# p loaded whole on two queues, zeros multiplied until it is there, the first product in passes, x scaled ahead of the evictions: the start and the end of a decoder block

## The chip, the cores and the metric

The kernel runs on one core of a Trainium2 chip. The core has a matrix engine (TensorE: PE for its products, PEld for its weight loads), a vector engine (DVE), a scalar engine (ACT), a general engine (POOL) and an engine that only issues transfers (SP). Transfers are issued from the queues of SP, ACT and POOL and share 16 DMA engines. The metric is the time of one execution on the device in microseconds (us): the median of several runs, lower is better.

## The reference

One layer of a hybrid decoder block on 512 rows (tokens) of 1024 numbers, in 32-bit floats. In short:

```python
hn = rmsnorm(x, g_mix)                                  # x: (512, 1024)
proj = hn @ w_in                                        # w_in: (1024, 14344), split into 13 parts
(xa, ba, ca, za, q, k, v, o, zb, ig, fg, ga, gb) = split(proj)
ya = ba * causal_short_conv(ca * xa, conv_w, conv_b)    # branch a
ya = (ya * silu(za)) @ w_a_out
hb = mlstm_chunkwise(q, k, v, ig + b_i, fg + b_f)       # branch b, 4 heads
yb = (sigmoid(o) * rmsnorm(hb, g_head) * silu(zb)) @ w_b_out
x = x + (sigmoid(ga) * ya + sigmoid(gb) * yb) @ w_o
gate = sigmoid(rmsnorm(x, g_ple) @ w_ple_gate)
x = x + gate * (p @ w_ple)                              # p: (512, 256), w_ple: (256, 1024)
return rmsnorm(x, g_final)
```

The change touches three pieces of it: the product `p @ w_ple`, which needs nothing but inputs and is computed first; the first rmsnorm of x; and the last rmsnorm with the stores of the result.

## The kernel before, in words

Every product is done in split precision: an operand becomes a high part (ACT copies it into a rounded type) and a low part (DVE or POOL subtracts the high part from the original), and each product is three matmuls, high by high, high by low and low by high (`mm3`, L205 to L207). Weights come in pieces of 128 x 4 x 512 numbers, 1 MB, in four buffers `wraw`, and are split into `whi` and `wlo` on the way (`split_half`, L152 and L153). The order of work on PE, ACT, DVE and POOL is written out by hand: each engine executes its instructions in the order of the program, and waits are put in where data or buffers ask for them. SP's queue holds the loads, each waiting for its buffer. SP and ACT share eight completion semaphores for their transfers, so the ninth transfer is issued only when the first has landed.

The start goes like this. `p` (tile `pin`, four row blocks t of 128 rows, 256 columns) is transposed on PE, in two halves k of 128 columns (`turn_p`, L485), split into `pT`, and multiplied with w_ple. w_ple is piece 0 of the weights; it comes in four quarters q = 2n + k, where n is the half of the 1024 output columns and k the half of the 256 rows. Each quarter is split on its own (`split_quarter`, L522 and L523): before the change the first two low parts are made on DVE and the other two on POOL. The product makes four banks of results for n = 0 (one per row block t), each of six matmuls, three per k. They are copied out to `ple` by `keep_ple` (L511 on DVE, L513 on ACT), and then the four banks are used again for n = 1; the first matmul into a bank waits for the copy out of it. Meanwhile x comes in four row blocks: ACT squares and sums each (`square_x`, L489), DVE and POOL form the reciprocal root (`power_x`, L492 and L493), and DVE scales the block in place (`scale_x`, L497 to L499). After the product with w_ple the scaled x is transposed (`turn_x`, L504) and split into `hn_hi` and `hn_lo`, the left operand of everything that follows. One matmul group of w_ple, (k = 1, t = 3) of n = 1, is kept for later and fills a wait between the transposes of x.

In the end, the last product gives the gate in column halves, the last row block (t = 3) in two quarter pieces. For each row block the gate is applied (`gated`, L1133 to L1135), the squares are summed (`squares`, L1138), the root is formed (`power` on DVE and POOL, L1164 and L1165; `final_scale`, L1169 to L1171), and both halves are scaled and stored (`final`, L1178 to L1183). All eight stores are issued on SP's queue.

Of the kernel before, what the change touches and what calls it, by code (L numbers as in the profile page):

```python
# [14 lines left out]
P = 128  # L15
S = 512
# [20 lines left out]
def hybrid_block(ctx, tc, x, p, g_mix, w_in, conv_w, conv_b, w_a_out, b_gates, g_head,  # L37
# [92 lines left out]
    def load_raw(between=None):  # L130
        i = state["raw"]
        state["raw"] += 1
        raws[i] = wraw.tile([P, HC, CW], F32, name=f"wraw{i}", tag="wraw")
        for src, ks, cs in chunks[i]:
            nc.sync.dma_start(raws[i][:, ks, cs], src)
            if between:
                between = between()
# [71 lines left out]
    def cut(hi, lo, src, scale=None):  # L209

        if scale is None:
            act.activation(hi, src, AF.Copy)
            dve.tensor_tensor(lo, src, hi.bitcast(F32), ALU.subtract)
        else:
            act.activation(hi, src, AF.Copy, scale=scale)
            dve.scalar_tensor_tensor(lo, src, scale, hi.bitcast(F32), ALU.mult, ALU.subtract)
# [226 lines left out]
    start_ctx, sp = open_pool("start")  # L443
    pin = sp.tile([P, NT, PLE], F32, name="pin", tag="hsf0", align_bytes=256)

    def load_p(k):
        nc.sync.dma_start(pin[:, :, k * P:(k + 1) * P],
                          p[0, 0, :, k * P:(k + 1) * P].rearrange("(t p) c -> p t c", p=P))

    load_p(0)  # L450
    load_raw(lambda: load_p(1))
# [8 lines left out]
    xin = sp.tile([P, NT, D], F32, name="xin", tag="xin")  # L460
    hnf = sp.tile([P, KT, S], F32, name="hnf")
    sq = hnf[:, 0:2, :].rearrange("p k s -> p (k s)")
    for t in range(NT):
        nc.sync.dma_start(xin[:, t, :], x[0, t * P:(t + 1) * P, :])
    nc.sync.dma_start(prow[0:8, :], g_mix[0].rearrange("(c p) -> c p", p=P))
    nc.sync.dma_start(prow[8:32, :], conv_w[0].rearrange("j (c p) -> (j c) p", p=P))
    nc.sync.dma_start(prow[32:40, :], conv_b[0].rearrange("(c p) -> c p", p=P))
    nc.sync.dma_start(prow[40:56, :], g_head[0].rearrange("(c p) -> c p", p=P))
    nc.sync.dma_start(prow[56:64, :], g_ple[0].rearrange("(c p) -> c p", p=P))
    load_raw()  # L470
    nc.sync.dma_start(wg_raw, w_in_v[:, :, IG:IG + 2 * NH])
    nc.sync.dma_start(bg, b_gates[0].rearrange("(g h) -> h g", g=2))

    prm = const.tile([P, 64], F32, name="prm")
    gm = prm[:, 0:8]
# [6 lines left out]
    def turn_p(k):  # L482
        pt = ps_x.tile([P, S], F32, name="ptp", tag="x")
        for t in range(NT):
            pe.transpose(pt[:, t * P:(t + 1) * P], pin[:, t, k * P:(k + 1) * P], ident)  # L485
        return pt

    def square_x(t):
        act.activation(sq, xin[:, t, :], AF.Square, accum_out=ss[:, t:t + 1])  # L489

    def power_x(t):
        dve.tensor_scalar(tmp[0][:, t:t + 1], ss[:, t:t + 1], 1.0 / D, EPS, ALU.mult, ALU.add)  # L492
        pool.tensor_tensor(tmp[1][:, t:t + 1], tmp[0][:, t:t + 1], mhalf[:, :1], ALU.pow)  # L493
# [25 lines left out]
    def split_quarter(q, e_lo):  # L519
        hi, lo = (u[:, q % HH, :] for u in splits[0][q // HH])  # L520
        raw = raws[0][:, q, :]
        act.activation(hi, raw, AF.Copy)  # L522
        e_lo.tensor_tensor(lo, raw, hi.bitcast(F32), ALU.subtract)  # L523

    for k in range(2):
        ptp = turn_p(k)
        split_quarter(k, dve)
        cut(pT[0][:, k, :], pT[1][:, k, :], ptp)
    split_quarter(2, pool)
    split_quarter(3, pool)  # L530
    state["split"] = 2
    del raws[0]
    for t in range(3):
        square_x(t)
    whi, wlo = ([splits[0][q // HH][u][:, q % HH, :] for q in range(4)] for u in range(2))
    state["use"] = 1
    splits.pop(0)
# [1 line left out]
    def ple_part(ps, n, k, t):  # L539
        mm3(ps, [u[:, k, t * P:(t + 1) * P] for u in pT], [whi[2 * n + k], wlo[2 * n + k]], k == 0, k == 1)  # L540

    pss = [bank(t) for t in range(NT)]
    for k in range(2):
        for t in range(NT):
            ple_part(pss[t], 0, k, t)
    for t in range(3):
        keep_ple(t, 0, pss[t], True)
        if t < 2:
            power_x(t)
    keep_ple(3, 0, pss[3])  # L550
    square_x(3)
    scale_x(0)
    power_x(2)
    scale_x(1)
    power_x(3)
    scale_x(2)
    scale_x(3)
    pss = [bank(t) for t in range(NT)]
    for k, t in [(0, 0), (0, 1), (0, 2), (0, 3), (1, 0), (1, 1), (1, 2)]:
# [613 lines left out]
    def final(t, n, on_act=False):  # L1173

        y = temp("sv"[n], "y")
        f = fs[:, t:t + 1]
        if n:
            dve.scalar_tensor_tensor(y, xr[:, t, half[1]], f, gfin[:, half[1]], ALU.mult, ALU.mult)  # L1178
# [4 lines left out]
        nc.sync.dma_start(out[0, t * P:(t + 1) * P, half[n]], y)  # L1183
# [27 lines left out]
    gated(pss[3][:, :CW // 2], 3, q[0])  # L1211
    squares(3, q[0], 1)
    final_scale(2)
    gated(psl[:, :CW // 2], 3, q[1])
    squares(3, q[1], 2)
    dve.tensor_scalar(base[:, 3:4], fss[:, 3, 1:2], 1.0 / D, base[:, 3:4], ALU.mult, ALU.add)
    final(2, 0)
    power(3, 2)
    final(2, 1)
    final_scale(3)  # L1220
    final(3, 0, True)
    final(3, 1)
# [23 lines left out]
```

## Time and profile before

| | |
|---|---|
| median of three runs | 870.08 us (869.50 to 870.92) |
| profiled execution, its own time | 871.68 us |
| its span | 869.7 us |
| PE busy | 852.3 us, 98% of the span |
| DVE, ACT, POOL busy | 599.8, 468.4, 255.8 us |
| bytes moved | 169.65 MB, mean 195 GB/s |
| PE's first product with w_ple | at 6.93 us |
| PE's last product | starts at 860.56 us |

The times in the rows that follow are microseconds from the start of the span. A row gives the start, the length, the engine, the line of the kernel, the operation, what it writes and reads, and, in brackets, how long the engine stood before it and what ended that. A matmul's length is its latency; what it costs in a row of matmuls is the distance to the next start. In the list of waits a row gives who waited for whom: the total, the number of waits and the longest. In the tables by stretch, each engine has its busy time and the number of instructions, then come the clock that TensorE was granted, the share of the DMA engines' time and GB/s.

### The profile page before, as it was taken

What the parts mean: (1) busy time and instruction counts of PE and PEld (TensorE: products, weight loads), DVE (VectorE), ACT (ScalarE), POOL (GpSimd) and SP (SyncE); (2) the same over time, 40 slices, a digit from 0 to 9 for tenths busy, and PEclk for the clock granted to TensorE, in tenths of its full rate; (3) what the DMA queues carried; (4) which work ended last, traced back from release to release, by engine and by line L of the source; (5) the groups of instructions that cost most, each with busy time, mean ns of one, the idle gap of its engine ahead of it and who ended that gap; (6) DMA issues with size and microseconds to landing.
All of it is one profiled execution on the core that took longest, in us unless ns stands there. A gap on an engine that the chain in (4) does not pass through costs nothing.

```text
span 869.7 us, 11799 instructions
## 1 busy us (share of the span) xinstructions
PE 852.3 (98%) x4507; PEld 732.3 (84%) x4507; DVE 599.8 (69%) x774; ACT 468.4 (54%) x674; POOL 255.8 (29%) x246
## 2 busy tenths in 40 slices
PE   7999999999999999999999999999999999999995
PEld 6877888888888888888888999999998888788885
DVE  4769676774674666755785588898986777864465
ACT  5575676555563755547656555545453256534342
POOL 3742422322333132331331424333410224030031
PEclk9999999999999999999999999999999999999999
DMA  8799996968855887867869989899898588994002
GB/s 289 262 210 220 275 221 127 223 233 193 177 163 145 191 176 158 238 193 158 236 122 269 230 192 163 202 181 181 181 326 309 97 194 211 272 329 157 1 1 97
DMA packets 100728, 169.65 MB, mean 195 GB/s; under 512 B 6272, under 2 KB 44224, under 8 KB 99392
## 3 DMA queue, kind: packets, MB, share of 16 engines
q0 software_dynamic: 39312, 76.03, 45.1%
q1 hardware_dynamic: 60208, 90.78, 31.5%
q10 hardware_dynamic: 1152, 2.10, 0.7%
q8 instruction: 35, 0.57, 0.3%
q14 instruction: 21, 0.17, 0.1%
HBM read 153.16 MB, written 15.73 MB: 194 GB/s over the span
## 4 chain that ended last, share of the span: by engine, by line
PE 80%; DMA 6%; issue 4%; DVE 4%; ACT 2%; POOL 2%; POOLq 0%; SPq 0%; DVEq 0%; ACTq 0%
PE mm L206 24%; PE mm L207 24%; PE mm L205 24%; DMA wraw<-in_w_in 3%; DMA wraw<-in_w_b_out 2%; DVE wlo L153 2%; PE pv L205 1%; ACT whi L152 1%; PE pv L206 1%; PE pv L207 1%; POOL wraw L159 1%; PE pty L744 1%; DMA sg_d<-c 1%; DMA pin<-in_p 0%; PE sc L207 0%
## 5 line engine op out<-in xcount | busy, mean ns | idle before, releaser
L153 DVE TENSOR_TENSOR wlo<-wraw,whi 128x1024 fp32r<-128x1024 f32 x234 | 299.1, 1281 | 127.3 <-ACT whi L152 127.0
L152 ACT ACTIVATE whi<-wraw 128x1024 fp32r<-128x1024 f32 x236 | 247.0, 1054 | 105.2 <-PE mm L207 44.7
L159 POOL DMA_DIRECT2D wraw<-in_w_in x110 | 136.0, 1402 | 289.1 <-DVE wlo L153 218.5
L205 PE MATMUL mm<-hn_hi,whi 128*128 128x256 f32 (+1 forms) x320 | 105.1, 328 | 0.0
L207 PE MATMUL mm<-hn_hi,wlo 128*128 128x256 f32 (+1 forms) x320 | 104.4, 326 | 0.2 <-POOL wlo L153 0.2
L206 PE MATMUL mm<-hn_lo,whi 128*128 128x256 f32 (+1 forms) x320 | 104.2, 326 | 0.0
L206 PE MATMUL mm<-wlo,hs 128*128 128x512 f32 x256 | 100.7, 393 | 1.1 <-DVE wlo L153 1.0
L205 PE MATMUL mm<-whi,hs 128*128 128x512 f32 x256 | 101.0, 394 | 0.3 <-DVE c L325 0.3
L207 PE MATMUL mm<-whi,hs 128*128 128x512 f32 x256 | 100.2, 391 | 0.0
L321 ACT ACTIVATE s<-mm 128x512 f32<-128x512 f32 x78 | 46.4, 595 | 94.6 <-PE mm L207 94.5
L206 PE MATMUL mm<-wlo,hn_hi 128*128 128x512 f32 x192 | 74.9, 390 | 0.2 <-DVE wlo L153 0.2
L205 PE MATMUL mm<-whi,hn_hi 128*128 128x512 f32 x192 | 75.0, 391 | 0.0
L207 PE MATMUL mm<-whi,hn_lo 128*128 128x512 f32 x192 | 74.8, 389 | 0.0
L207 PE MATMUL mm<-hs,wlo 128*128 128x256 f32 x256 | 72.5, 283 | 0.8 <-DVE wlo L153 0.8
L205 PE MATMUL mm<-hs,whi 128*128 128x256 f32 x256 | 72.5, 283 | 0.0
L206 PE MATMUL mm<-hs,whi 128*128 128x256 f32 x256 | 72.4, 283 | 0.0
L207 PEld LDWEIGHTS mm<-hn_hi,wlo 128*128 128x128 f32 x320 | 60.9, 190 | 5.7 <-POOL wlo L153 0.8
L206 PEld LDWEIGHTS mm<-hn_lo,whi 128*128 128x128 f32 x320 | 60.9, 190 | 4.7
L205 PEld LDWEIGHTS mm<-hn_hi,whi 128*128 128x128 f32 x320 | 60.9, 190 | 4.6
L206 PEld LDWEIGHTS mm<-wlo,hs 128*128 128x128 f32 x256 | 48.5, 190 | 11.9 <-DVE wlo L153 2.4
L205 PEld LDWEIGHTS mm<-whi,hs 128*128 128x128 f32 x256 | 48.5, 189 | 10.8 <-DVE c L325 0.7
L207 PEld LDWEIGHTS mm<-whi,hs 128*128 128x128 f32 x256 | 48.5, 189 | 10.1
(276 smaller groups left out, 1680.0 us busy)
## 6 DMA issues: line engine op xcount, KB each, us to landing
wraw<-in_w_in SPq DMA_DIRECT2D x32, 1024.0 KB, 6.1
wraw<-in_w_in POOLq DMA_DIRECT2D x62, 512.0 KB, 6.8
wraw<-in_w_in SPq DMA_DIRECT2D x48, 512.0 KB, 4.5
wraw<-in_w_in POOLq DMA_DIRECT2D x48, 256.0 KB, 5.8
wraw<-in_w_b_out SPq DMA_DIRECT2D x8, 1024.0 KB, 6.4
wraw<-in_w_b_out POOLq DMA_DIRECT2D x16, 512.0 KB, 7.4
yt_d<-yc POOLq DMA_DIRECT2D x4, 1024.0 KB, 7.6
wraw<-in_w_a_out SPq DMA_DIRECT2D x4, 1024.0 KB, 8.9
```

Of the source, the lines that this page charges most:

```text
L152: act.activation(hi, t, AF.Copy)
L153: (e_lo or dve).tensor_tensor(lo, t, hi.bitcast(F32), ALU.subtract)
L159: nc.gpsimd.dma_start(raws[to][:, ks, cs], src[:, ks, :], accum_op=ALU.add)
L205: pe.matmul(ps, lhsT=a[0], rhs=b[0], start=first, stop=False, **kw)
L206: pe.matmul(ps, lhsT=a[0], rhs=b[1], start=False, stop=False, **kw)
L207: pe.matmul(ps, lhsT=a[1], rhs=b[0], start=False, stop=last, **kw)
L321: act.activation(to[i], src, AF.Copy, scale=scale)
L744: pe.transpose(pts[v][:, t * P:(t + 1) * P], y[:, t, v * P:(v + 1) * P], ident)
```

## The change

At the start, p is loaded whole as two transfers of two row blocks each, one on SP's queue and one on ACT's, ahead of everything else. The first transposed half of `hn_lo`, not used yet, is filled with zeros by DVE, and PE multiplies these zeros six times into a spare bank ahead of the transposes of p, and once more after them. w_ple's quarters 0 and 1 are loaded next, then x's blocks 0 and 1, w_ple's quarters 2 and 3, and x's blocks 2 and 3. The seven small loads (five parameter vectors, the gate columns of w_in, the gate biases) move from SP's queue to POOL's. For k = 0 of n = 0 the product is done pass by pass: four matmuls of high by high, four with the low part of p, four with the low part of w_ple. The high part of p's first half is made on DVE instead of ACT, and all four low parts of w_ple on DVE. x's blocks 0 and 1 are squared by ACT before w_ple's quarters 2 and 3 are split, and scaled by DVE before the banks of n = 0 are copied out. At the end, outputs that ACT makes are stored from ACT's queue; the right half of row block 2 is finished before the last quarter of the gate, and its left half moves to ACT.

```diff
+    p_v = p[0, 0].rearrange("(t p) c -> p t c", p=P)
+    for i, queue in enumerate((nc.sync, nc.scalar)):
+        queue.dma_start(pin[:, 2 * i:2 * i + 2, :], p_v[:, 2 * i:2 * i + 2, :])
...
+    def load_ple(n):
+        for src, ks, cs in chunks[0][2 * n:2 * n + 2]:
+            nc.sync.dma_start(raws[0][:, ks, cs], src)
+
+    load_ple(0)
+
+    dve.memset(hn_lo[:, 0, :].bitcast(F32), 0.0)
+    warm = ps_x.tile([P, S], F32, name="warm", tag="x")
+
+    def keep_warm(n):
+        for _ in range(n):
+            pe.matmul(warm, lhsT=hn_lo[:, 0, :P], rhs=hn_lo[:, 0, :], start=True, stop=True)
+
+    keep_warm(6)
...
-    for t in range(NT):
-        nc.sync.dma_start(xin[:, t, :], x[0, t * P:(t + 1) * P, :])
-    nc.sync.dma_start(prow[0:8, :], g_mix[0].rearrange("(c p) -> c p", p=P))
...
+    for i in range(2):
+        for t in range(2 * i, 2 * i + 2):
+            nc.sync.dma_start(xin[:, t, :], x_v[:, t, :])
+        if i == 0:
+            load_ple(1)
     load_raw()
...
+    nc.gpsimd.dma_start(prow[0:8, :], g_mix[0].rearrange("(c p) -> c p", p=P))
...
+    nc.gpsimd.dma_start(wg_raw, w_in_v[:, :, IG:IG + 2 * NH])
+    nc.gpsimd.dma_start(bg, b_gates[0].rearrange("(g h) -> h g", g=2))
...
-    for k in range(2):
-        ptp = turn_p(k)
-        split_quarter(k, dve)
-        cut(pT[0][:, k, :], pT[1][:, k, :], ptp)
-    split_quarter(2, pool)
-    split_quarter(3, pool)
...
+    ptp = turn_p(0)
+    dve.tensor_copy(pT[0][:, 0, :], ptp)
+    hi, lo, raw = quarter(0)
+    act.activation(hi, raw, AF.Copy)
+    low(pT[0][:, 0, :], pT[1][:, 0, :], ptp)
+    low(hi, lo, raw)
+    ptp = turn_p(1)
+    keep_warm(1)
+    split_quarter(1, dve)
+    cut(pT[0][:, 1, :], pT[1][:, 1, :], ptp)
+    for t in range(2):
+        square_x(t)
+        power_x(t)
+    for q in (2, 3):
+        split_quarter(q, dve)
+    for t in range(2):
+        scale_x(t)
...
-    for k in range(2):
+    for i, (a, b) in enumerate(((pT[0], whi), (pT[1], whi), (pT[0], wlo))):
         for t in range(NT):
-            ple_part(pss[t], 0, k, t)
+            pe.matmul(pss[t], lhsT=a[:, 0, t * P:(t + 1) * P], rhs=b[0], start=i == 0, stop=False)
+    for t in range(NT):
+        ple_part(pss[t], 0, 1, t)
+    square_x(2)
     for t in range(3):
         keep_ple(t, 0, pss[t], True)
-        if t < 2:
-            power_x(t)
+        if t == 0:
+            power_x(2)
...
-        nc.sync.dma_start(out[0, t * P:(t + 1) * P, half[n]], y)
+        (nc.scalar if on_act else nc.sync).dma_start(out[0, t * P:(t + 1) * P, half[n]], y)
...
     final_scale(2)
+    final(2, 1)
     gated(psl[:, :CW // 2], 3, q[1])
+    final(2, 0, True)
     squares(3, q[1], 2)
     dve.tensor_scalar(base[:, 3:4], fss[:, 3, 1:2], 1.0 / D, base[:, 3:4], ALU.mult, ALU.add)
-    final(2, 0)
     power(3, 2)
-    final(2, 1)
```

Two places show how this moves instructions. The first is DVE in the start, from its second low part of p on (`pT`, the second one) to its second copy out of a bank (`COPY ple`); `wlo` is a low part of w_ple, `rtmp` are the small columns of the reciprocal root, `xin` is x. Before:

```order
L213 TENSOR_TENSOR pT_135<-ptp,pT_134 128x512
L511 COPY ple_144<-mm 128x512
L492 TENSOR_SCALAR rtmp_141<-ss 128x1
L511 COPY ple_145<-mm 128x512
L492 TENSOR_SCALAR rtmp_141<-ss 128x1
L511 COPY ple_146<-mm 128x512
L497 SCALAR_TENSOR_TENSOR rtmp_143<-rtmp_142,rtmp_141 128x1
L498 TENSOR_SCALAR rtmp_143<-rtmp_143 128x1
L499 TENSOR_SCALAR xin<-xin,rtmp_142,rtmp_143 128x1024
```

And now:

```order
L213 TENSOR_TENSOR pT_141<-ptp,pT_140 128x512
L510 TENSOR_SCALAR rtmp_147<-ss 128x1 x2
L541 TENSOR_TENSOR wlo_181<-wraw_129,whi_180 128x512 x2
L515 SCALAR_TENSOR_TENSOR rtmp_149<-rtmp_148,rtmp_147 128x1
L516 TENSOR_SCALAR rtmp_149<-rtmp_149 128x1
L517 TENSOR_SCALAR xin<-xin,rtmp_148,rtmp_149 128x1024
L515 SCALAR_TENSOR_TENSOR rtmp_149<-rtmp_148,rtmp_147 128x1
L516 TENSOR_SCALAR rtmp_149<-rtmp_149 128x1
L517 TENSOR_SCALAR xin<-xin,rtmp_148,rtmp_149 128x1024
L529 COPY ple_150<-mm 128x512
L510 TENSOR_SCALAR rtmp_147<-ss 128x1
L529 COPY ple_151<-mm 128x512
```

Between the last low part of p and the first copy out of a bank DVE now has two small steps, two low parts of w_ple and two scalings of x, where before it had nothing. On ACT the squares of x's first two blocks (`hnf,ss<-xin`) have moved ahead of the last two splits of w_ple (`whi`), which those low parts need. ACT in the start before, and after it now:

```order
L522 ACTIVATE whi_170<-wraw_128 128x512
L212 ACTIVATE pT_134<-ptp 128x512
L522 ACTIVATE whi_170<-wraw_128 128x512
L212 ACTIVATE pT_134<-ptp 128x512
L522 ACTIVATE whi_172<-wraw_128 128x512 x2
L489 ACTIVATE hnf,ss<-xin 128x1024 x3
L513 ACTIVATE ple_147<-mm 128x512
```

```order
L448 DMA pin<-in_p 128x2x256
L553 ACT_TABLE_LOAD
L553 ACTIVATE whi_178<-wraw_129 128x512
L540 ACTIVATE whi_178<-wraw_129 128x512
L212 ACTIVATE pT_140<-ptp 128x512
L507 ACTIVATE hnf,ss<-xin 128x1024 x2
L540 ACTIVATE whi_180<-wraw_129 128x512 x2
L507 ACTIVATE hnf,ss<-xin 128x1024 x2
L531 ACTIVATE ple_153<-mm 128x512
```

The second place is ACT in the end, from the sigmoid of the last quarter (`e<-mml`) on; `c,fss<-xr` are the squares, `y<-xg` is an output. Before:

```order
L1133 ACTIVATE e<-mm,er 128x256
L1138 ACTIVATE c,fss<-xr 128x256
L1133 ACTIVATE e<-mml,er 128x256
L1138 ACTIVATE c,fss<-xr 128x256
L1180 ACTIVATE y<-xg,fs 128x512
```

And now:

```order
L1167 ACTIVATE e<-mm,er 128x256
L1172 ACTIVATE c,fss<-xr 128x256
L1167 ACTIVATE e<-mml,er 128x256
L1214 ACTIVATE y<-xg,fs 128x512
L1217 DMA out<-y 128x512
L1172 ACTIVATE c,fss<-xr 128x256
L1214 ACTIVATE y<-xg,fs 128x512
L1217 DMA out<-y 128x512
```

An output and its store now stand ahead of the last squares, and the last store of ACT's output follows on ACT's own queue.

More of the change, by code (lines that the diff above doesn't have):

```diff
@@ L444, in hybrid_block @@
     pin = sp.tile([P, NT, PLE], F32, name="pin", tag="hsf0", align_bytes=256)
[L446 to L451, printed above, removed]
+    p_v = p[0, 0].rearrange("(t p) c -> p t c", p=P)
+    for i, queue in enumerate((nc.sync, nc.scalar)):
+        queue.dma_start(pin[:, 2 * i:2 * i + 2, :], p_v[:, 2 * i:2 * i + 2, :])
+    state["raw"] = 1
+    raws[0] = wraw.tile([P, HC, CW], F32, name="wraw0", tag="wraw")
+    def load_ple(n):
[8 more added lines that the diff above has]
+    keep_warm(6)
     pT = [sp.tile([P, 2, S], F32R, name=f"pT{i}", tag="pT" if i else "hsf1", align_bytes=256) for i in range(2)]
@@ L462, in hybrid_block @@
     sq = hnf[:, 0:2, :].rearrange("p k s -> p (k s)")
-    for t in range(NT):
-        nc.sync.dma_start(xin[:, t, :], x[0, t * P:(t + 1) * P, :])
-    nc.sync.dma_start(prow[0:8, :], g_mix[0].rearrange("(c p) -> c p", p=P))
[L466 to L469, printed above, removed]
-    load_raw()
-    nc.sync.dma_start(wg_raw, w_in_v[:, :, IG:IG + 2 * NH])
-    nc.sync.dma_start(bg, b_gates[0].rearrange("(g h) -> h g", g=2))
+    x_v = x[0].rearrange("(t p) d -> p t d", p=P)
+    for i in range(2):
[3 more added lines that the diff above has]
+            load_ple(1)
+    load_raw()
+    nc.gpsimd.dma_start(prow[0:8, :], g_mix[0].rearrange("(c p) -> c p", p=P))
+    nc.gpsimd.dma_start(prow[8:32, :], conv_w[0].rearrange("j (c p) -> (j c) p", p=P))
+    nc.gpsimd.dma_start(prow[32:40, :], conv_b[0].rearrange("(c p) -> c p", p=P))
+    nc.gpsimd.dma_start(prow[40:56, :], g_head[0].rearrange("(c p) -> c p", p=P))
+    nc.gpsimd.dma_start(prow[56:64, :], g_ple[0].rearrange("(c p) -> c p", p=P))
+    nc.gpsimd.dma_start(wg_raw, w_in_v[:, :, IG:IG + 2 * NH])
+    nc.gpsimd.dma_start(bg, b_gates[0].rearrange("(g h) -> h g", g=2))
     prm = const.tile([P, 64], F32, name="prm")
@@ L523, in split_quarter, with quarter, low @@
         e_lo.tensor_tensor(lo, raw, hi.bitcast(F32), ALU.subtract)
-    for k in range(2):
-        ptp = turn_p(k)
-        split_quarter(k, dve)
-        cut(pT[0][:, k, :], pT[1][:, k, :], ptp)
-    split_quarter(2, pool)
-    split_quarter(3, pool)
+    def quarter(q):
+        hi, lo = (u[:, q % HH, :] for u in splits[0][q // HH])
+        return hi, lo, raws[0][:, q, :]
+    def low(hi, lo, src):
+        dve.tensor_tensor(lo, src, hi.bitcast(F32), ALU.subtract)
+    ptp = turn_p(0)
[15 more added lines that the diff above has]
+        scale_x(t)
     state["split"] = 2
     del raws[0]
-    for t in range(3):
-        square_x(t)
     whi, wlo = ([splits[0][q // HH][u][:, q % HH, :] for q in range(4)] for u in range(2))
@@ L542, in hybrid_block @@
     pss = [bank(t) for t in range(NT)]
-    for k in range(2):
+    for i, (a, b) in enumerate(((pT[0], whi), (pT[1], whi), (pT[0], wlo))):
         for t in range(NT):
-            ple_part(pss[t], 0, k, t)
+            pe.matmul(pss[t], lhsT=a[:, 0, t * P:(t + 1) * P], rhs=b[0], start=i == 0, stop=False)
+    for t in range(NT):
+        ple_part(pss[t], 0, 1, t)
+    square_x(2)
     for t in range(3):
         keep_ple(t, 0, pss[t], True)
-        if t < 2:
-            power_x(t)
+        if t == 0:
+            power_x(2)
+    square_x(3)
+    scale_x(2)
     keep_ple(3, 0, pss[3])
[L551 to L554, printed above, removed]
     power_x(3)
-    scale_x(2)
     scale_x(3)
```

## The prediction

> **What bounds the kernel now.** I read the page's busy row first, then PE's list of waits, then the first 25 us and the last 10 us in order of time.
>
> ```profile
> PE 852.3 (98%) x4507; PEld 732.3 (84%) x4507; DVE 599.8 (69%) x774; ACT 468.4 (54%) x674; POOL 255.8 (29%) x246
> ```
>
> ```profile
> PE ptp L485 <- DMA pin<-in_p: 5.1, 2, 3.6
> PE mm L206 <- DVE wlo L153: 1.9, 3, 1.0
> PE mm L207 <- DVE wlo L153: 0.8, 1, 0.8
> ```
>
> PE is busy for 852.3 of 869.7 us, and 5.1 us of what is left is its wait for p. From there to its last product it stands for only some 3 us. So what the start gains or loses reaches the end nearly whole, and the middle, which the change leaves in its order on PE, DVE and ACT, is taken as unchanged. Only the start and the tail after PE's last product are in play. Here is PE in the start (time, length), and two pieces of the chain of waits where the spacing of the products changes:
>
> ```profile
> 3.58 1.09 PE L485 MATMUL ptp<-ident,pin 128*128 128x128 f32 x4 [3.58 <-DMA pin<-in_p]
> 6.16 1.12 PE L485 MATMUL ptp<-ident,pin 128*128 128x128 f32 x4 [1.50 <-DMA pin<-in_p]
> 6.93 0.78 PE L205 MATMUL mm<-whi,pT 128*128 128x512 f32 x1
> 11.97 0.42 PE mm L207
> 12.39 0.23 PE mm L205
> 19.53 0.39 PE L207 MATMUL mm<-whi,pT 128*128 128x512 f32 x1
> ```
>
> The first half of p is there at 3.58, the second at 6.16. The products with w_ple begin at 6.93, at 0.43 us each; from about 12.2 they take 0.23. Of 48, 45 run back to back: 24 for the left half of the columns, then 21 for the right half, the last from 19.53. After it come the transposes of x, the next weights and everything else. **So 19.53 is the mark to beat.** Before, PE alone sets it. The other engines in the same stretch:
>
> ```profile
> 7.36 0.63 ACT L522 ACTIVATE whi<-wraw 128x512 fp32r<-128x512 f32 x1 [0.85 <-DMA wraw<-in_w_ple]
> 7.89 0.58 ACT L212 ACTIVATE pT<-ptp 128x512 fp32r<-128x512 f32 x1
> 10.44 1.06 ACT L489 ACTIVATE hnf<-xin 128x1024 f32<-128x1024 f32 x1 [0.66 <-DMA xin<-in_x]
> 11.79 1.06 ACT L489 ACTIVATE hnf<-xin 128x1024 f32<-128x1024 f32 x1 [0.20 <-DMA xin<-in_x]
> 13.06 1.06 ACT L489 ACTIVATE hnf<-xin 128x1024 f32<-128x1024 f32 x1
> 8.02 0.69 DVE L523 TENSOR_TENSOR wlo<-wraw,whi 128x512 fp32r<-128x512 f32 x1 [0.68 <-ACT whi L522]
> 8.63 0.68 DVE L213 TENSOR_TENSOR pT<-ptp,pT 128x512 fp32r<-128x512 f32 x1
> 13.12 0.69 DVE L511 COPY ple<-mm 128x512 f32<-128x512 f32 x1 [3.81 <-PE mm L207]
> 13.73 0.14 DVE L492 TENSOR_SCALAR rtmp<-ss 128x1 f32<-128x1 f32 x1
> 13.81 0.69 DVE L511 COPY ple<-mm 128x512 f32<-128x512 f32 x1
> 15.12 0.21 DVE L497 SCALAR_TENSOR_TENSOR rtmp<-rtmp,rtmp 128x1 f32<-128x1 f32 x1
> 16.28 0.15 DVE L492 TENSOR_SCALAR rtmp<-ss 128x1 f32<-128x1 f32 x1
> 2.73 0.95 POOL L480 MEMSET wg<- 128x1024 f32 x1
> 11.72 1.67 SPq L135 DMA_DIRECT2D wraw<-in_w_in  x2
> ```
>
> Starts of neighbours give the pace: a split on DVE 0.61 us (8.02 to 8.63), an eviction 0.61 (13.12 to 13.73), scaling one row block of x 1.16 (15.12 to 16.28), squaring one on ACT 1.27 (11.79 to 13.06), a split on ACT 0.53 (7.36 to 7.89).
>
> **The change, part by part.**
>
> *p and the zeros.* p comes in 1 KB runs on two queues instead of two halves of 512-byte runs. Bounds for its arrival are 3.58, when half is there now, and 6.16. I take 4.4: the second quarter MB adds some 0.9 us at the rate of the first. Eight transposes (2.2 us at the cold pace of 1.09 for four) and one product of zeros bring the first real product to about 7.0, as before. The six products of zeros run while PE stood anyway; at 0.43 each they end near 4 if the memset that feeds them is done by 1.4. They cost nothing, and if p came at 3.6 they would cost 0.4. If they make the array fast earlier, at most 12 x 0.20 = 2.4 us of the slow products go. **But I count nothing for that, because PE no longer sets the mark.**
>
> *What does.* The first product of the right half writes the bank that the first eviction empties. Before, that copy was DVE's next work at 13.12, far ahead of PE. Now DVE does two splits (q = 2, 3, taken from POOL) and two scalings of x first, and the splits follow, on ACT, the squares of two blocks of x. From X, the arrival of the second block of x: ACT squares it (1.27 to the next instruction), splits q = 2 (0.63), and two hand-overs cost 0.06: DVE starts at X + 1.96. Then 0.61 + 0.61 + 1.16 + 1.16 + 0.69 = 4.23 to the end of the first copy. PE then needs 20 x 0.227 = 4.54 to the start of its last product, plus 0.07 for hand-overs. The last product starts at X + 1.96 + 4.23 + 4.54 + 0.07 = X + 10.80. It equals 19.53 at X = 8.73.
>
> *X.* x's second block is now the last byte of the first 2 MB; before, the first block was, and was used at 10.44. That is one bound. DMA did this on the way:
>
> ```profile
> 2.00:6.75 4.75, 1.68 (x7) 1.31 (x8) 0.70 (x2) 1.13 (x3) 1.68 (x3) 1.00 0.82 240
> 6.75:10.00 3.25, 3.25 (x10) 2.64 (x9) 1.88 (x3) 2.37 (x4) 0.78 (x1) 1.00 1.03 400
> ```
>
> (last column GB/s.) The first 1.1 MB went at 240 GB/s and took 4.75 us; at 400 they take 2.85, so the other bound is X = 10.44 - 1.9 = 8.5. The slow stretch is the time of the 512-byte runs and of what queued behind them; those runs are now half as many and twice as long, but nothing shows that they alone were its cause. I take X = 9.1, nearer to the full rate. ACT allows it: w_ple's second quarter at about 6.5 (7.36 now, for the same first MB) plus a split and p's cut make it free for the first square at 7.6, and 7.8 + 1.27 is 9.1. **Start: 9.1 + 10.80 = 19.90, 0.4 us later than 19.53**; with both bounds -0.2 to +1.7.
>
> *POOL.* Seven small loads go to POOL's queue ahead of its memset and of the powers that the scalings need. Nearest rows:
>
> ```profile
> L159 POOL DMA_DIRECT2D wraw<-in_w_in x110 | 136.0, 1402 | 289.1 <-DVE wlo L153 218.5 <-DVE cv L373 43.8 <-DMA wraw<-in_w_in 10.5
> L1080 POOL DMA_DIRECT2D gfin<-in_g_final x1 | 0.5, 528 | 0.5 <-DMA xr<-in_x 0.5
> ```
>
> Seven at 0.53 are 3.7 us, at 1.40 9.8. From 2.73 on, where the memset (0.95) stood that they now precede, POOL is free between 7.4 and 13.5, and the first power (0.54) is done by 7.9 to 14.0; the scalings want it at X + 1.96 + 1.22 = 12.3. So the cover is there in all but the dearest case; without it up to 1.7 us more. I take zero. The small loads also leave SP's queue, where weights stood behind them; those weights were not late before.
>
> *The tail.* The last quarter block, to the end:
>
> ```profile
> 858.88 0.54 POOL L1165 TENSOR_TENSOR etmp<-etmp,mhalf 128x1 f32<-128x1 f32 x1 [5.23 <-DVE etmp L1164]
> 860.87 0.47 ACT L1133 ACTIVATE e<-mml,er 128x256 f32<-128x256 f32 x1 [0.44 <-PE mml L207]
> 861.84 0.42 DVE L1135 TENSOR_TENSOR xr<-xr,e 128x256 f32<-128x256 f32 x1
> 862.36 0.42 ACT L1138 ACTIVATE c<-xr 128x256 f32<-128x256 f32 x1 [1.01 <-DVE xr L1135]
> 863.03 0.74 DVE L1178 SCALAR_TENSOR_TENSOR y<-xr,fs,gfin 128x512 f32<-128x512 f32 x1
> 863.19 0.98 POOL L1165 TENSOR_TENSOR etmp<-etmp,mhalf 128x1 f32<-128x1 f32 x1 [3.78 <-DVE etmp L1164]
> 864.85 0.75 DVE L1178 SCALAR_TENSOR_TENSOR y<-xr,fs,gfin 128x512 f32<-128x512 f32 x1
> L1183 SPq DMA_DIRECT2D out<-y x4: 333/333/382, 862.8 to 866.1; - x4
> ```
>
> ```profile
> 480.57 0.33 ACTq L716 DMA_DIRECT2D sg_d<-sg  x1
> 480.95 1.07 ACT L152 ACTIVATE whi<-wraw 128x1024 fp32r<-128x1024 f32 x1 [0.40 <-ACT sg L715]
> ```
>
> ACT now does one output of block 2 (0.72) and its store between 861.34 and the last square: 861.37 + 0.72, a store that holds ACT 0.40 as in the second fence, so the square starts at 862.49 instead of 862.36: +0.13. The power on POOL took 0.98 beside DVE's output at 863.03, and 0.54 at 858.88; that output now comes before 861.3, while DVE waits for ACT's sigmoid at 860.87: -0.43. The two last stores leave from two queues at about 865.4 instead of the last at 866.1 from one: the scalings end 0.30 earlier and 0.4 of queueing behind the other store goes. **Tail: -0.7**, between -0.2 (if POOL keeps its 0.98) and -0.9.
>
> The Trainium skill bears this out ("SBUF — State Buffer", Who interferes with whom): a DVE instruction with two SBUF inputs blocks a GpSimd instruction that reads SBUF. The trace agrees, 0.98 against 0.54. By the rule the whole 0.43 comes back, which is the -0.7; without it the tail is -0.3.
>
> **Sum.** 0.4 - 0.7 = -0.3 on the profiled execution: span 869.7 to 869.4, its time 871.68 to 871.4. The median shown is 870.08, 1.6 under the profiled execution; the same difference gives **869.8**.
>
> **Rivals.**
>
> *Faster (20%).* The start is at its floor and the middle gives something too: w_in's first pieces, issued at 11.72 behind the small loads, go out sooner, so some of the 2.7 us that PE waits for DVE's splits could go. Floor: -0.2 - 0.9, and 1.5 of the waits: 867.5. For it: SP's queue stalls less. Against: those waits name DVE, not a DMA. That PE sets the mark, fast from the first product (7.0 + 44 x 0.227 = 17.0, 2.5 us less), needs DVE's copy by 12.4, so X near 6.2: two us under the bound above.
>
> The Trainium skill speaks against that case as well ("TensorE: Matmul & The Clock Gate", Part 4: PE-mode transpose): transposes do not count as work that wakes the clock. By it the zeros' 2.6 us, broken by transposes, are too short, and with the 3.4 us that the page gives as the window (its Part 1) the first products stay slow to about 10.4: an estimated 0.9 us less, not 2.5. Here the slow pace lasts some 5 us beyond the transposes at 6.16, which agrees but proves nothing.
>
> *Late data (12%).* Three queues now share the 16 engines, and POOL's loads cut w_in's gate columns into 32-byte pieces just while x comes. From X = 11.2 on it decides (2.5 - 0.7 = 1.8 us more than before), and X = 11.5 gives 2.8 - 0.7, 872.2. For: the slow stretch is unexplained. Against: fewer pieces in p.
>
> *The array falls asleep (8%).* If it is fast early, the left half ends at 7.0 + 24 x 0.227 = 12.5, and PE then stands 2.8 us until the first copy (15.3). If the clock drops there, some 16 products cost 0.20 more: 3.2 - 0.3, 873.0. At the end the clock does drop when PE stands (column before the DMA share; PE's last product ended before 860.87):
>
> ```profile
> 865.00:866.00 1.00, 0.00 (x0) 0.00 (x0) 0.59 (x1) 0.61 (x1) 0.00 (x0) 0.80 0.32 121
> 866.00:867.00 1.00, 0.00 (x0) 0.00 (x0) 0.00 (x0) 0.00 (x0) 0.00 (x0) 0.50 0.53 201
> ```
>
> 0.80 over 865 to 866 puts the drop at 865.6, 4.8 us after, more than 2.8: hence the small chance.
>
> **How the numbers follow.** 60% stay for the forecast, whose own range is 869.0 to 871.6 (start -0.2 to +1.7, tail -0.9 to -0.2). With the rivals' times the range is 867.2 to 872.6. A measurement of this kernel tells 0.2%, 1.7 us, from no change: below 868.3 is faster, above 871.8 slower. The forecast lies inside; the first rival gives faster 20%, the other two slower 20%.
>
> **What would show it.** The first copy of evictions ends near 15.3, and PE has a gap of 0.3 to 3 us before the right half, released by DVE's copy; the last product with w_ple starts within 0.5 us of 19.9. If that gap is absent, my reading of the bank wait is wrong. X is the start of ACT's second square, near 9.1. In the tail, POOL's last power takes 0.55 and the two last stores start within 0.1 us of each other. The forecast falls if the first copy ends before 13.5 or after 17.

## The result and the profile after

The changed kernel takes 872.79 us (median of 22 executions, 870.11 to 875.32), the kernel before, on the same chip, 870.14 (868.38 to 873.80): a ratio of 1.0026, 95% interval 1.0015 to 1.0038. It is **slower by 2.3 us** by that ratio (2.65 by the medians); its median lies 3.0 us above the forecast's 869.8 and just above the range of 867.2 to 872.6. Two slow executions, one of 2201 us (the one profiled in the first set of the copies ahead of the scaling, below) and one of 1429 us (the kernel before), are left out of the ratios. The profiled execution has a span of 872.3 us instead of 869.7.

PE in the start of the changed kernel, in order of time:

```profile
1.48 2.93 PE L463 MATMUL warm<-hn_lo 128*128 128x512 f32 x6 [1.48 <-DVE hn_lo L458]
4.60 1.94 PE L503 MATMUL ptp<-ident,pin 128*128 128x128 f32 x8 [0.19 <-DMA pin<-in_p]
6.19 0.73 PE L463 MATMUL warm<-hn_lo 128*128 128x512 f32 x1
6.75 1.99 PE L579 MATMUL mm<-whi,pT 128*128 128x512 f32 x8
...
15.77 0.47 PE L205 MATMUL mm<-whi,pT 128*128 128x512 f32 x1 [3.40 <-DVE rtmp L510]
...
16.77 0.45 PE L206 MATMUL mm<-wlo,pT 128*128 128x512 f32 x1
17.02 0.63 PE L207 MATMUL mm<-whi,pT 128*128 128x512 f32 x1
17.45 0.63 PE L205 MATMUL mm<-whi,pT 128*128 128x512 f32 x1
...
20.01 0.57 PE L205 MATMUL mm<-whi,pT 128*128 128x512 f32 x1
20.42 0.39 PE L206 MATMUL mm<-wlo,pT 128*128 128x512 f32 x1
...
22.05 0.39 PE L207 MATMUL mm<-whi,pT 128*128 128x512 f32 x1
```

The wait for p is gone, and the left half runs at the fast pace from its first product (eight in 1.99 us). Then PE stands for 3.40 us, and after five fast products it is **slow again**: 0.43 us apart from 17.02 to 20.4. The last product with w_ple starts at 22.05 instead of 19.53. The granted clock (the column before the DMA share) says what the slow stretch is:

```profile
13.60:15.70 2.10, 0.00 (x0) 0.00 (x0) 2.03 (x7) 1.95 (x5) 0.00 (x0) 1.00 1.09 349
15.70:17.00 1.30, 1.23 (x5) 1.05 (x6) 1.30 (x3) 0.21 (x1) 0.55 (x1) 0.99 1.09 348
17.00:20.40 3.40, 3.40 (x9) 2.67 (x8) 2.22 (x7) 0.00 (x0) 0.55 (x1) 0.50 1.08 362
20.40:24.00 3.60, 3.60 (x23) 2.88 (x22) 0.24 (x2) 2.82 (x5) 0.60 (x1) 1.00 1.05 387
```

The clock was halved for 3.4 us, and this began 1.2 us after PE had resumed. It was halved once more in this profile, far from the start, behind two waits of PE for the splits of a weight (0.83 and 0.76 us):

```profile
750.80:754.20 3.40, 1.81 (x7) 0.95 (x7) 1.90 (x3) 2.95 (x3) 0.12 (x1) 1.00 1.09 264
754.30:757.70 3.40, 3.40 (x9) 2.62 (x8) 3.40 (x5) 2.20 (x3) 0.57 (x1) 0.50 1.10 283
```

What PE waited for in the start, on ACT, DVE and POOL:

```profile
9.69 1.06 ACT L507 ACTIVATE hnf<-xin 128x1024 f32<-128x1024 f32 x1 [0.30 <-DMA xin<-in_x]
10.75 1.14 ACT L540 ACTIVATE whi<-wraw 128x512 fp32r<-128x512 f32 x2
```

```profile
11.40 1.29 DVE L541 TENSOR_TENSOR wlo<-wraw,whi 128x512 fp32r<-128x512 f32 x2 [0.37 <-ACT whi L540]
...
14.21 0.81 DVE L517 TENSOR_SCALAR xin<-xin,rtmp,rtmp 128x1024 f32<-128x1024 f32 x1
14.94 0.68 DVE L529 COPY ple<-mm 128x512 f32<-128x512 f32 x1
```

```profile
7.12 0.97 POOL L498 MEMSET wg<- 128x1024 f32 x1
9.73 0.57 POOL L511 TENSOR_TENSOR rtmp<-rtmp,mhalf 128x1 f32<-128x1 f32 x1 [1.64 <-DVE rtmp L510]
```

The first copy ends at 15.62, as the order of DVE's work has it. POOL is through its seven small loads and its memset at 8.1, before the first power is wanted. The tail:

```profile
863.58 0.28 PE L207 MATMUL mml<-whi,h 128*128 128x256 f32 x1
863.90 0.47 ACT L1167 ACTIVATE e<-mml,er 128x256 f32<-128x256 f32 x1 [0.44 <-PE mml L207]
...
865.40 0.42 ACT L1172 ACTIVATE c<-xr 128x256 f32<-128x256 f32 x1 [0.42 <-DVE xr L1169]
...
866.24 0.54 POOL L1199 TENSOR_TENSOR etmp<-etmp,mhalf 128x1 f32<-128x1 f32 x1 [3.80 <-DVE etmp L1198]
...
867.45 0.75 DVE L1212 SCALAR_TENSOR_TENSOR y<-xr,fs,gfin 128x512 f32<-128x512 f32 x1
```

From the start of PE's last product to the end of the span: 872.3 - 863.58 = 8.72, before 869.7 - 860.56 = 9.14. So the span's +2.6 is +2.5 in the start, +0.5 between (with one halving there in each of the two profiles: at 754.3 here, at 83.9 before), -0.4 in the tail.

### The profile page after: what moved, and what is told of

Same layout as the page of the kernel before. It is cut to its first block, busy times and chain, and to the rows that moved or that the text cites. A ratio compares the mean times of both kernels' runs of the same rounds, so it can differ in the third digit from the quotient of the medians.

```text
span 872.3 us, 11824 instructions
## 1 busy us (share of the span) xinstructions
PE 854.9 (98%) x4514; PEld 734.0 (84%) x4514; DVE 601.8 (69%) x777; ACT 468.6 (54%) x674; POOL 257.9 (30%) x251
## 4 chain that ended last, share of the span: by engine, by line
PE 83%; DVE 5%; DMA 4%; issue 3%; ACT 2%; POOL 1%; SPq 0%; ACTq 0%; POOLq 0%; DVEq 0%
PE mm L207 25%; PE mm L205 25%; PE mm L206 25%; DMA wraw<-in_w_b_out 2%; DVE wlo L153 2%; DMA wraw<-in_w_in 1%; ACT whi L152 1%; PE pv L205 1%; PE pv L206 1%; PE pv L207 1%; DMA xin<-in_x 1%; PE pty L778 1%; PE sc L207 1%; PE sc L206 1%; PE sc L205 1%
```

## The experiments

The theory: the copies of the left half stand behind the scaling of x; PE stands, which costs its own time, and the standing halves the clock, which costs 1.6 us more. The rivals: late data (x, three queues) and a half pace with some other cause. Times are medians of 12 executions (11 in one set) beside the kernel before on the same chip. For each kernel the mean granted clock of every execution is known too. The profiles say how to read it: the seven without a halving ahead of PE's last product have 0.996 to 0.998, the three with one 0.995 or 0.996, the three with two 0.993. So 0.995 or less means a halving, but not where in the kernel it was, and some halvings are missed. Of the kernel before, 32 of 97 executions have 0.995 or less; they took 871.9 us in the mean, the other 65 869.1.

**Fourteen more products of zeros while PE stands.** The wait stays, the standing goes.

```diff
     for t in range(NT):
         ple_part(pss[t], 0, 1, t)
+    keep_warm(14)
     square_x(2)
```

> The changed kernel with fourteen more products of zeros (3.2 us) between the left and the right half, where PE stands; nothing else. Theory (the clock is halved because PE stands there): the right half still starts near 15.8, since DVE's first copy is no earlier, but all its products take 0.23, the granted clock is 1.00 through 17.0 to 20.4, and the last product starts near 20.4 instead of 22.05: 1.6 us less, time 871.2. Rival (the half pace has another cause, such as the transfers that run beside): the eight slow products stay, the last product at 22.05 or later, time 872.8 or more.

Measured: 870.86 against 869.65, ratio 1.0007 (0.9993 to 1.0021). PE's rows and the clock in the same stretch:

```profile
12.02 3.33 PE L463 MATMUL warm<-hn_lo 128*128 128x512 f32 x14
15.56 0.47 PE L205 MATMUL mm<-whi,pT 128*128 128x512 f32 x1 [0.21 <-DVE rtmp L510]
```

```profile
17.00:20.40 3.40, 3.40 (x16) 2.63 (x14) 2.07 (x5) 1.05 (x2) 0.55 (x1) 1.00 1.08 364
```

The right half starts as late as before, the clock stays at 1.00 with the same transfers beside it, and the last product starts at 20.20. One execution of 12 has a clock of 0.995 or less; of the changed kernel's 22 it is 19. Against 1.0026 that is 1.6 us, as expected. The two intervals overlap a little, so it is the rows and the clocks that show it: the standing, not the data, halves the clock.

**No products of zeros at all.**

```diff
-    keep_warm(6)
...
-    keep_warm(1)
```

> The changed kernel without any products of zeros, the six ahead of p and the one after. Theory: PE starts slow, the left half ends some 1.5 to 2.5 us later (13.7 to 14.9 instead of 12.4), which takes this time from the gap only, since the first copy of the left half waits for DVE's scaling until 15.0 anyway; PE then stands 1 to 2 us, too little to halve the clock, and the last product starts near 20.4 instead of 22.05: without zeros the kernel is 1.6 us FASTER, 871.2. Rival (a fast array early is worth something here): as slow as the changed kernel, 872.8, or slower by up to 2.

Measured: 871.64 against 869.65, ratio 1.0016 (1.0005 to 1.0027).

```profile
6.32 3.75 PE L577 MATMUL mm<-whi,pT 128*128 128x512 f32 x8
...
15.75 0.47 PE L205 MATMUL mm<-whi,pT 128*128 128x512 f32 x1 [1.88 <-DVE rtmp L509]
```

```profile
13.70:17.10 3.40, 1.52 (x7) 1.16 (x7) 3.29 (x10) 2.05 (x5) 0.55 (x1) 0.99 1.10 349
17.10:20.50 3.40, 3.40 (x10) 2.66 (x9) 2.13 (x6) 0.00 (x0) 0.55 (x1) 0.51 1.08 365
```

The array is slow at first (eight products in 3.75 us) and PE's wait shrinks to 1.88, but the last product still starts at 22.01: the fast left half was worth nothing. The time lies between the expected 871.2 and the rival's 872.8. A miss in one part: 1.88 us of standing, which I had called too little, halved the clock in this profile, and 7 of 12 executions have 0.995 or less. (Its mean clock is 0.993, with a second halving at 754.3 as in the changed kernel.) In the 3.4 us ahead of the halving PE had products for 1.52 us. So it need not stand for a whole such stretch; about half of one without products seems enough.

**Four products of zeros.** This tests that reading with the standing at 2.3 us.

```diff
+    keep_warm(4)
     square_x(2)
```

> The changed kernel with four products of zeros (0.9 us) behind the left half, so that PE stands 2.5 us instead of 3.4. My forecast's reading (the clock drops only 4.8 us after PE stops) and the reading that a whole window of 3.4 us must be empty say: never halved, granted clock 0.997 in all executions, time as with fourteen zeros, 1.6 us less than the changed kernel. Theory now (a window that is more than half empty is enough, and where the windows lie is chance): halved in about 2.5/3.4, three of four executions, which then show 0.993 to 0.995; time 0.4 us less than the changed kernel, 872.3 beside 870.1 of before.

Measured: 871.12 against 870.20, ratio 1.0019 (1.0001 to 1.0037); 9 of 12 executions at 0.995 or less.

```profile
13.60:17.00 3.40, 1.44 (x6) 1.23 (x7) 3.28 (x10) 1.82 (x5) 0.55 (x1) 1.00 1.09 348
17.00:20.40 3.40, 3.40 (x9) 2.66 (x8) 2.06 (x5) 0.00 (x0) 0.55 (x1) 0.50 1.08 366
```

Three of four, as expected. The share of low clocks rises with the standing: 1 of 12 at 0.2 us, 7 of 12 at 1.9, 9 of 12 at 2.3, 19 of 22 at 3.4. With so few executions the last three are not told apart, and the kernel before, which has no such gap, has a third; the first against the last is clear. The time alone would not have told it (0.6 us less than the changed kernel, within the intervals).

**The copies ahead of the scaling,** in two sets of runs.

```diff
-    for t in range(2):
-        scale_x(t)
     state["split"] = 2
...
     square_x(3)
-    scale_x(2)
+    for t in range(3):
+        scale_x(t)
     keep_ple(3, 0, pss[3])
```

> The changed kernel, but DVE copies three banks of the left half out before it scales blocks 0 and 1 of x; the two low parts of w_ple stay ahead of the copies. Theory (what costs is that the copies stand behind the scaling): DVE's low parts end near 12.6 as in the changed kernel, the first copy ends near 13.3 instead of 15.6, PE stands about 1.1 us instead of 3.4, the clock is granted whole through 17 to 20.4, the last product with w_ple starts near 18.0 instead of 22.05, and the transposes of x, which then wait for the scaling of block 3, start near 19.4 instead of 22.57. Time 3 us less than the changed kernel, 869.8. Rival (the loss comes from late x or from the three queues): the gap stays over 2 us and the time within 1 us of the changed kernel.

> The kernel with the copies ahead of the scaling once more, to see in its profile where the 2 to 3 us went that its time did not gain. Theory now (a window of about 3.4 us in which PE has products for less than half of the time halves the clock for the next one; transposes don't count): PE stands about 1.1 us before the right half, which is harmless, but again about 1 us before the transposes of x, which last 1.5 us, and the clock is 0.50 for 3.4 us somewhere from 18 to 25. Granted clock at 0.993 to 0.995 in most executions. Rival (another engine): the clock is 1.00 there and PE has a new wait of 2 us, for a low part of w_in from POOL or for ACT's copies.

Measured: 872.29 (11 executions) against 869.65, ratio 1.0015 (0.9998 to 1.0031), and 870.24 against 870.20, ratio 1.0007 (0.9987 to 1.0028). The rows are those of the second set.

```profile
14.38 0.50 PE L205 MATMUL mm<-whi,pT 128*128 128x512 f32 x1 [0.70 <-DVE ple L529]
...
18.92 0.55 PE L522 MATMUL pt<-ident,xin 128*128 128x128 f32 x3
20.45 1.20 PE L522 MATMUL pt<-ident,xin 128*128 128x128 f32 x9 [0.99 <-DVE xin L517]
```

The last product starts at 18.39, but x's block 3 is scaled only by 20.4, because DVE waits 0.96 us for ACT's square and 0.66 us for POOL on the way, which my sum of 19.4 left out. The gain is smaller than the 3 us I expected: by the ratios 1.0 and 1.7 us less than the changed kernel, the first within the 1 us that the rival of late data allowed. In the two sets, 14 of 23 executions have low clocks, and this profile does not show where.

**The same with zeros ahead of the transposes of x,** to see whether it is there.

```diff
+    keep_warm(7)
     pt = ps_x.tile([P, S], F32, name="pt", tag="x")
     pe.transpose(pt[:, :64], prow, ident[:64, :64])
```

> The kernel with the copies ahead of the scaling, plus seven products of zeros (1.6 us) behind the right half, where PE waits for the scaling of x's block 3 (0.99 us, in the middle of the first transposes, in its profile). In two sets of runs 14 of 23 of its executions had a granted clock of 0.995 or less, 20 of 63 of the kernel before. Theory (there it is the 2.8 us without products around the transposes of x that sometimes halve the clock): with the zeros about a third of the executions at 0.995 or less, as before; transposes of x from about 20.4 as without; 1 us less in the mean, near 870.0 beside 870.1 of before. Rival (its low clocks come from elsewhere): more than half still at 0.995 or less and 870.9 or more.

Measured: 870.96 against 869.80, ratio 1.0013 (0.9997 to 1.0029); 4 of 12 at 0.995 or less. The share is the expected one, the time is the rival's (870.9 or more), and the profile shows another place:

```profile
13.91 0.47 PE L205 MATMUL mm<-whi,pT 128*128 128x512 f32 x1 [2.13 <-DVE ple L529]
```

```profile
11.40:14.80 3.40, 1.27 (x5) 0.48 (x3) 2.38 (x6) 2.35 (x5) 0.72 (x2) 0.98 1.03 365
14.80:18.20 3.40, 3.10 (x8) 2.42 (x8) 3.26 (x9) 1.39 (x3) 0.39 (x1) 0.52 1.09 348
```

Here PE stands 2.13 us ahead of the right half even with the copies first, since DVE's low parts, which precede them, wait for x's arrival through ACT's squares; and the clock is halved from about 14.7 (worked out from the 0.98). X's second block was squared at 10.15 here, at 9.00 in the profile of the same order without zeros, so late data is part of this gap. Where the other low clocks of this order fall stays open; with 12 executions each, 14 of 23 and 4 of 12 do not tell the two places apart.

**The tail alone,** on the kernel before: the last hunks of the change (stores of ACT's outputs from ACT's queue, `final(2, 1)` ahead of the last quarter of the gate, `final(2, 0, True)` behind it).

```diff
+    final(2, 1)
     gated(psl[:, :CW // 2], 3, q[1])
+    final(2, 0, True)
     squares(3, q[1], 2)
...
-    final(2, 0)
     power(3, 2)
-    final(2, 1)
```

> The kernel before with only the end of the change: ACT's outputs stored from ACT's queue, block 2's right half ahead of the last quarter of the gate, its left half on ACT. My forecast had -0.7 us for this; the two profiles side by side (from the start of PE's last product to the end of the span) say -0.42. Theory: 8.7 us from PE's last product instead of 9.14, time 869.7 against 870.1. Rival (nothing or a loss): 870.1 or more.

Measured: 867.98 against 869.65, ratio 0.9984 (0.9969 to 0.9999): faster.

```profile
860.00 0.54 POOL L1165 TENSOR_TENSOR etmp<-etmp,mhalf 128x1 f32<-128x1 f32 x1 [3.83 <-DVE etmp L1164]
```

From PE's last product (857.31) to the end of the span (865.8) it takes 8.49 us; in nine profiles with this tail 8.49 to 8.74, in four with the old one 9.09 to 9.14: -0.4 us. The measured gain, 1.4 us by the ratio, is more than that, and its interval reaches down to 0.1. Part of the rest may be chance in the clock: 2 of its 12 executions have 0.995 or less, beside a third of before's, which at 871.9 against 869.1 us would be some 0.5 us (an estimate). The remainder is not explained.

This kernel has the old start, and in its profile the last product with w_ple starts at 18.06, not 19.53:

```profile
18.06 0.39 PE L207 MATMUL mm<-whi,pT 128*128 128x512 f32 x1
18.38 0.27 PE L562 MATMUL pt<-ident,prow 64*128 64x64 f32 x1
```

**The kernel before, three times more,** unchanged, for its start alone.

> The kernel before, unchanged: another execution, for its start alone. My forecast took the start of its last product with w_ple, 19.53 in the one profile shown, as the mark to beat. Theory now: when the slow pace of the first products ends is chance (12.2 in that profile, 9.4 in the profile of the kernel with the new end, whose start is the same), so the mark lies anywhere from 17.7 to 19.6, 18.6 in the mean, with 0.46 us for every us that the fast pace comes earlier. Rival: 12.2 and 19.53 within 0.2, and the other profile is the exception.

> The same again: the mark anywhere from 17.7 to 19.6 by the theory, 19.53 within 0.2 by the rival.

> The same again: the mark anywhere from 17.7 to 19.6 by the theory, 19.53 within 0.2 by the rival.

The five profiles of this start and, for the tail, how long after PE's last product ended the granted clock fell (worked out from its mean over the microsecond in which it falls):

| profile | first product | fast from | slow products | last product with w_ple | clock falls after the end |
|---|---|---|---|---|---|
| shown with the forecast | 6.93 | 12.2 | 12 | 19.53 | 4.8 us |
| tail alone | 6.75 | 9.4 | 6 | 18.06 | 5.1 us |
| first repeat | 7.09 | 10.2 | 7 | 18.63 | 2.3 us |
| second repeat | 6.86 | 11.1 | 9 | 18.91 | 2.3 us |
| third repeat | 6.86 | 11.0 | 9 | 18.82 | 1.9 us |

The mark is 18.8 in the mean, and 19.53 was the latest of five. In all thirteen profiles the clock fell 1.9 to 5.3 us after PE's last product. The row for the fall in the first repeat, where PE's last product starts at 857.47:

```profile
860.00:861.00 1.00, 0.00 (x0) 0.00 (x0) 0.69 (x2) 0.00 (x0) 0.90 (x1) 0.53 0.43 170
```

**No wait at all between the halves.** Blocks 0 and 1 of the right half go to two spare banks, and the copies of the left half are shared between ACT and DVE.

```diff
+    for t in range(2, NT):
+        keep_ple(t, 0, pss[t])
     square_x(2)
...
+    for t in range(2):
+        keep_ple(t, 0, pss[t], True)
-    pss = [bank(t) for t in range(NT)]
-    for k, t in [(0, 0), (0, 1), (0, 2), (0, 3), (1, 0), (1, 1), (1, 2)]:
+    pss = [ps_x.tile([P, S], F32, name="mmx", tag="x") for _ in range(2)] + [bank(t) for t in range(2, NT)]
+    for k, t in [(0, 0), (1, 0), (0, 1), (1, 1), (0, 2), (1, 2), (0, 3)]:
         ple_part(pss[t], 1, k, t)
+    warm = ps_x.tile([P, S], F32, name="warm2", tag="x")
+    for _ in range(6):
+        pe.matmul(warm, lhsT=hn_lo[:, 0, :P], rhs=hn_lo[:, 0, :], start=True, stop=True)
```

> The changed kernel, with the right half's blocks 0 and 1 in two spare banks, so that its first twelve products wait for no copy; blocks 2 and 3 of the left half are copied by ACT ahead of its squares of x's blocks 2 and 3, blocks 0 and 1 by DVE after all scaling; the right half goes block by block, and six products of zeros fill PE's wait ahead of the transposes of x. Theory: no gap behind the left half, last product with w_ple starts near 17.0 (22.05 in the changed kernel, 19.53 before), x's block 3 is scaled by 18.6 and the transposes of x start near 18.7 (22.57 and 20.05), clock 1.00 throughout: 3.9 us less than the changed kernel, 1.4 + 0.4 less than the kernel before, 868.0 to 868.4. Rival (the next wait, for POOL's low part of w_in or for DVE's low parts, takes the gain): transposes early, but 869.7 or more.

Measured: 868.94 against 870.20, ratio 0.9990 (0.9966 to 1.0013). The last product with w_ple starts at 16.50 and the transposes of x at 18.38, as expected, but the time lies between the expected 868.0 to 868.4 and the rival's 869.7. The split of what the transposes give waits for the parameters:

```profile
19.84 0.22 DVE L600 COPY prm<-pt 128x64 f32<-128x64 f32 x1
```

```profile
20.15 1.84 ACT L215 ACTIVATE hn_hi<-pt,prm 128x512 fp32r<-128x512 f32 x3 [2.04 <-DVE prm L600]
```

**That wait taken out too:** against the kernel with spare banks, the parameter rows are transposed and copied right behind the left half, the root of x's block 3 is begun before block 2 is scaled, and there are four products of zeros instead of six.

```diff
...
     power_x(2)
+    keep_ple(0, 0, pss[0], True)
     square_x(3)
-    scale_x(2)
+    pt = ps_x.tile([P, S], F32, name="pt", tag="x")
+    pe.transpose(pt[:, :64], prow, ident[:64, :64])
+    dve.tensor_copy(prm, pt[:, :64])
     power_x(3)
+    scale_x(2)
     scale_x(3)
...
```

> The kernel with spare banks, shortened where its profile still had waits: the parameter rows are transposed and copied right behind the left half (there the split of the first transposed x waited for that copy until 19.84), the root of x's block 3 is begun before block 2 is scaled (it waited 0.66 us for POOL behind it), left block 0 is copied in a wait of DVE, and four products of zeros instead of six. Theory: x's block 3 scaled near 17.8 instead of 18.7, transposes of x from near 17.9 (18.38 in the kernel with spare banks, 20.05 in the profile of before), first high part of hn near 18.3 instead of 20.15; 1 to 1.8 us less than the kernel with spare banks, 867.2 to 868.0 beside 870.1 of before. Rival (w_in's first pieces are the next wait): early transposes, then as much longer a wait for a low part of w_in, and 868.9 as with spare banks.

Measured: 868.71 against 870.08, ratio 0.9975 (0.9958 to 0.9993): faster than both kernels.

```profile
18.64 1.85 ACT L215 ACTIVATE hn_hi<-pt,prm 128x512 fp32r<-128x512 f32 x3 [0.52 <-PE pt L522]
```

The high parts come 1.5 us sooner than with spare banks. The time is 0.2 us less by the medians and 1.3 by the ratios (the two were measured on different chips, and their intervals overlap), with the median above the expected 867.2 to 868.0; and as it has the new tail too, its interval overlaps that of the tail alone. That a better start adds to the better tail is likely from the rows, not shown by the times.

## Why the prediction was wrong

**What held.** p at 4.60 (forecast 4.4), the first product at 6.75 (7.0), PE no longer setting the mark, POOL's queue at no cost, and the zeros of no use (22.01 without them, 22.05 with). Whether the zeros cost anything stays open: without them the time is 0.9 us less by the ratios (1.0016 and 1.0026, with intervals that overlap), and PE stands for less. The chain through DVE held closest: x's block 1 at 9.69 gives 9.69 + 10.80 = 20.49 without halving, and with the clock kept up and x there at 9.48 it was 20.20 (sum 20.28). X itself, 9.1 in the forecast, was 0.6 late, inside its bounds. In the middle no change is seen: from the last product with w_ple to PE's last product, five profiles of before's start took 838.8 to 842.9 us, and five of the changed kernel and its variants (no zeros, four, fourteen, copies first) 838.8 to 841.9; only the copies with seven zeros, which stand in that stretch, took 843.4. The spread of 4 us inside both is larger than the +0.5 of the one pair of profiles.

**The step that failed: the sum put the halved clock behind the gap at nothing, and left it to the rival "the array falls asleep" at 8%.** The forecast had the gap (2.8 us; it was 3.4) and the mechanism, and dismissed it because the clock fell 4.8 us after PE's last product in the profile's end. That was one draw: in the thirteen profiles it is 1.9 to 5.3 us. The rows fit a clock that is decided over stretches of 3.4 us, so that the halving comes at a stretch's end, which may lie after PE has resumed: here 1.2 us after. In all three profiles where this gap halved the clock, PE had products for 1.2 to 1.5 of the 3.4 us ahead of it. The profile of before had the same thing, unread, in its middle, with a wait of only 0.98 us:

```profile
81.63 0.50 PE L206 MATMUL mm<-wlo,hs 128*128 128x512 f32 x1 [0.98 <-DVE wlo L153]
...
82.99 0.78 PE L685 MATMUL ptc<-ident,rows 4*128 4x4 f32 x10
83.64 0.39 PE L687 MATMUL ptc<-ident,rows 4*128 4x4 f32 x4
```

```profile
83.90:87.30 3.40, 3.40 (x10) 2.71 (x10) 3.33 (x6) 1.31 (x2) 0.58 (x1) 0.51 0.99 373
```

The wait and a microsecond of small transposes left 1.5 us of products in the 3.4 before 83.9. The same wait (0.99 and 0.96 us) and the same transposes stand in the first two repeats, with no halving there, which fits that it hangs on where the stretches lie. So the price of a gap is the price of a halving, 8 products at 0.20 more (the forecast had 16), times a chance that grows with the gap, and for 2.8 us that chance is far from 8%. That this rival's own figure, 873.0, which lay outside the stated range, is 0.2 from the measured median is luck: it counted 16 slow products where there were 8, and started from the early x and the base that are taken up below.

The Trainium skill ("TensorE: Matmul & The Clock Gate", Part 1: The HAM clock gate) speaks of a free-running window of about 3.4 us and of a return to half rate after an idle window. The length agrees (3.4 us at 0.50) and so does the chance in where the windows lie: that page gives 6, 11 or 14 slow products for one kernel, here there were 6 to 12. That a window must be idle the runs do not bear out: 1.88 us of standing was enough in one profile. Its Part 4 (PE-mode transpose), that transposes do not count as work, fits the halving at 83.9, where the transposes are of 4 columns; the forecast's conclusion from it, slow products to 10.4, was wrong, as eight products took 1.99 us from 6.75. Nor does the profile of the copies first fit it, if its stretches are as long as a halved one (3.413 us in the clock record of the changed kernel's trace) and are counted back from the fall at its end, 864.1:

```profile
17.61:21.02 3.41, 2.42 (x15) 1.65 (x14) 2.19 (x6) 2.19 (x4) 1.81 (x2) 1.00 1.07 371
21.02:24.43 3.41, 3.41 (x24) 2.92 (x22) 2.25 (x4) 3.41 (x7) 3.41 (x3) 1.00 1.05 388
```

Of the 2.42 us only 1.2 are products, fewer than ahead of most halvings here; some 1.1 are eight transposes of 128 x 128, and no halving follows. So whole transposes seem to count; one profile does not show it for sure.

**The base.** The forecast compared with 19.53 and then took 1.6 us off for the median. But that profile was long partly because its array woke late (19.53 against 18.8 in the mean) and its clock was halved at 83.9. The change takes the late waking away, and with it what made the profile longer than the median. Against the mean, the start without any halving costs 20.2 to 20.5 less 18.8, 1.4 to 1.7 us, not 0.4; 0.7 of the difference is the mark, the rest x's later arrival.

**The tail, mis-sized: -0.7, was -0.4.** POOL's power took 0.54 instead of 0.98, all of the gain. From the start of DVE's last output to the end it is 869.7 - 864.85 = 4.85 before and 872.3 - 867.45 = 4.85 after: the second queue for the last store gave none of its 0.4, and ACT's output in front of the square cost none of its 0.13 (the square starts 1.50 after ACT's sigmoid, 1.49 before).

**The sum, mended:** 1.4 to 1.7 for the copies behind the scaling, 1.6 to 1.85 (20.20 to 22.05) for the halving times the some 0.8 of executions that have it there (19 of 22 low clocks, where about a third would have one anyway), 0.4 off in the tail: 2.3 to 2.8 us. This is an estimate made with the result in hand, and the 0.8 takes the low clocks for halvings in the start. Measured: 2.3 in the kernel's own set of runs (1.3 to 3.3 by the interval).

## What to carry to other kernels

In these runs a wait on the matrix engine cost twice: its length, and a chance of 3.4 us at half clock behind it, which was greater the longer PE stood; filling an unavoidable wait with products of zeros keeps the clock, and here it gave back 1.6 us. Before copies out of result banks are put behind other work, count who writes those banks next, or take a spare bank. And what hangs on where the clock's windows lie (the first fast product, the moment of a halving) is read from several profiles, since one shows one draw.

## What was not expected of the hardware

- The clock was halved only after PE had resumed (resumed at 15.77, halved 17.0 to 20.4), and after waits as short as 0.98 us with 14 small transposes beside them. In the thirteen profiles it happened in three places: behind the gap of the start, at those small transposes (83.9 here, 86.3 in one other profile) and behind waits for split weights near 750 us (three profiles). The last two come in some profiles of the same instructions and not in others.
- The wake-up is chance as well: the same start had 6, 7, 9, 9 and 12 slow products, which moved its last product with w_ple between 18.06 and 19.53. The granted clock reads 1.00 in that first slow stretch (the prediction's row of 6.75 to 10.00), while a later halving reads 0.50.
- The kernel's middle varied by 4 us from one profile to the next, with PE's waits for late splits of weights. In the second repeat PE waited 3.5 us in five waits where the third had 1.7 in two:

```profile
PE mm L206 <- DVE wlo L153: 3.5, 5, 1.0
PE mm L205 <- ACT whi L152: 1.4, 1, 1.4
```
